# Block products by Strassen's scheme for the dense projections of a hybrid decoder step on one core

## The chip, the cores and the metric

The kernel runs on one core of a Trainium2 chip. The metric is the device time of one launch in microseconds; the time given for a kernel is the median of its runs. A profile is one execution of the program, whose span is read from the trace. Engines are named as the profile names them: PE (matrix multiplication, with PEld for its weight loads), DVE (vector), ACT (scalar activation), POOL (GpSimd) and SP (the queue that issues most DMA).

## The reference, cut to what matters

The computation is one inference step of a decoder with two layers. There are 2048 prompt tokens and 8 x 4 = 32 sample tokens, with D_MODEL = 1024. Everything is float32.

```python
def even_mixer(h, w_in, b_fox, lb, hgrn_gain, w_out, hgrn_s0, fox_attend):      # layer 0
    proj = h @ w_in                                                              # 1024 x 4100
    qa, fa, ia, ga, qb, kb, vb, gb, fb = _split(proj, [A_WIDTH] * 4 + [B_WIDTH] * 4 + [B_HEADS])
    f = lb + (1.0 - lb) * jax.nn.sigmoid(fa)
    o_a, s_a = gated_linear_chunked(ha(qa), ha(1.0 - f), ha(ia), ha(jnp.log(f)), hgrn_s0)
    o_a = head_rmsnorm(o_a, hgrn_gain) * jax.nn.silu(ga)
    log_fb = jax.nn.log_sigmoid(fb + b_fox)
    o_b = fox_attend(hb(qb), kb_h, vb_h, log_fb) * jax.nn.silu(gb)
    return jnp.concatenate([o_a, o_b], axis=-1) @ w_out, ...                     # 1024 x 1024

def odd_mixer(h, w_in, w_gate, b_gate, gla_gain, w_out, gla_s0):                 # layer 1
    q, k, v, g, r = _split(h @ w_in, ...)                                        # 1024 x 3088
    log_f = jax.nn.log_sigmoid(r @ w_gate + b_gate) / GLA_GATE_NORMALIZER
    o, s = gated_linear_chunked(hk(q) * C_KEY_DIM ** -0.5, hk(k), hv(v), hk(log_f), gla_s0)
    return (head_rmsnorm(o, gla_gain) * jax.nn.silu(g)) @ w_out, s               # 1024 x 1024

def run_trunk(x, ...):
    for l in range(2):
        x = x + mixer(rmsnorm(x, norm[l]), ...)
    return rmsnorm(x, final_norm), ...
```

The prompt's forgetting attention ("fox") is causal over its own 2048 tokens; a sample's looks back on 2048 cached tokens of a paged cache. The four dense products, w_in and w_out of both layers, are what the change is about.

## The kernel before, in words

**Stages.** The prompt is taken in two halves of 1024 tokens; the 32 sample tokens ride with half 0. `phase_even` runs the input projections of layer 0 for half 0 and then half 1, mixed with the linear attention of its heads (`lin_attn`). `phase_fox` runs the forgetting attention. `phase_odd` runs, for each half, the output projection of layer 0, the norm, the input projections of layer 1 with their linear attention, and the output projection of layer 1, and at the end the final norm.

**Units.** A dense product is cut into units of 256 output columns: 16 in the even layer's input, 4 in its output, 12 in the odd layer's input, 4 in its output. Each runs once for each half, 72 runs in all. Half of the units are token-major (`proj_tm`, L491): 128 tokens are the stationary operand, 256 weight columns move, and the result has tokens on partitions. The others are feature-major (`proj_fm`, L482): 128 weight columns are stationary and the tokens move, in three segments of 352 in half 0 (1024 + 32 tokens) and two of 512 in half 1.

**Three products.** Both operands are kept as a float16 high part and low part; `mm3` (L476) multiplies high x high, high x low and low x high into one sum in PSUM. A unit has 8 such steps along the 1024 inputs.

```python
    def mm3(self, ps, lh, rh, first, last):
        nc.tensor.matmul(ps, lh[0], rh[0], start=first, stop=False)
        nc.tensor.matmul(ps, lh[0], rh[1], start=False, stop=False)
        return nc.tensor.matmul(ps, lh[1], rh[0], start=False, stop=last)
```

**Weights.** `half_unit` (L315) has four steps: fetch the float32 columns by DMA; `measure` their largest value (DVE, L292); derive a power of two as `scale`; and `split` them into a high and a low part. Of the four parts of a unit, two have their low part made by DVE (L346) after one ACT operation (L345), two by POOL (L353) after two of ACT (L351, L352). The split is made anew in each half. `later_unit` measures the 20 units of the later projections during even half 1. `staged` (L1070) runs the units in order and, as products go by, takes the steps of the next three units.

**Activations.** `act` is one tile of 128 partitions x (high, low) x 8 x 1056 float16, in a single buffer. It is filled by `norm_groups` (L408: row scaling L428 on DVE, transposes on PE, then high part L473 on ACT and low part L474 on DVE) or, for the output projections, by `y_pieces` and `y_to_act` (L1632 on ACT, L1633 on DVE) from the attention outputs `yT` in DRAM. `handover` (L452) interleaves this with the last unit of the old and the first unit of the new activations.

**Sample tokens in token-major units.** `few_rows` (L510) multiplies the 32 tokens in four column strips of PE, each with two of the eight steps; ACT and DVE add up the four strips (L525, L527).

**Order of work.** `mux` weaves two generators by costs in nanoseconds that each step yields; a scheduler then settles each engine's order. SP issues nearly all DMAs in order. PSUM has three buffers (`pj`) for projections.

Of the kernel before, what the change touches and what calls it, by code (L numbers as in the profile page):

```python
# [19 lines left out]
P = 128  # L20
# [10 lines left out]
WU = 272  # L31
LAG_N = 2
ASK = 0
# [6 lines left out]
EWR = 3  # L40
# [4 lines left out]
TAG1 = "o"  # L45
# [8 lines left out]
WSPLIT = 4  # L54
FOX_S = 411000.0
# [5 lines left out]
YPOOL = (2, 6)  # L61
# [4 lines left out]
SCALE = 128.0 ** -0.5  # L66
LEVELS = (1, 2, 4, 8, 16, 32, 64)
# [46 lines left out]

class Parts(tuple):
# [6 lines left out]
class Kern:  # L122
# [6 lines left out]
    def consts(self):  # L129
# [17 lines left out]
        self.kc, self.n_kc, self.scales = cp.tile([P, 184], F32, name="kc"), 0, {}  # L147
        self.vmax = cp.tile([P, NPG], F32, name="vmax")
# [8 lines left out]
        self.x1d = dp.tile([NTOK, D], F32, name="x1d")  # L157

# [85 lines left out]
    def gain_scale(self, g, pps, tag, nm):  # L244


        out = self.kcol(2)
        self.power2(self.spread(g, pps, tag, nm), 2.0**8, out)
        self.nc.vector.tensor_scalar(g, g, out[:, 0:1], None, ALU.mult)
        return out  # L250

    def kcol(self, n=1):
        self.n_kc += n
        assert self.n_kc <= 184
        return self.kc[:, self.n_kc - n : self.n_kc]
# [28 lines left out]
    def unit_scale(self, key, parts, rm, pool, pps, nm, undo, k):  # L284
# [3 lines left out]
        def measure():  # L288
            if key in self.scales:
                return  # L290
            for a, r in enumerate(parts()):
                nc.vector.tensor_reduce(rm()[:, a : a + 1], r, mybir.AxisListType.XY, ALU.max,  # L292
                                        apply_absolute_value=True)
            nc.vector.reduce_max(rm()[:, WSPLIT:], rm()[:, :WSPLIT], axis=mybir.AxisListType.X)

        def scale():
            if key in self.scales:
                return
            sc = self.scales[key] = self.kcol(3)
            self.power(rm()[:, WSPLIT:], 2.0**14, sc, pool, pps, nm)  # L300
            if undo is not None:
                self.last_scale = nc.vector.tensor_scalar(sc[:, 2:3], sc[:, 1:2], undo[:, 1:2], k, ALU.mult, ALU.mult)
# [3 lines left out]
    @staticmethod  # L306
    def sources(w, cols, h):

        for a in range(WSPLIT):
            off = 0  # L310
            for c, n in cols:
                yield a, off, n, w[a * h * P : (a + 1) * h * P, c : c + n].rearrange("(k p) c -> p k c", p=P)
                off += n

    def half_unit(self, pool, pps, w, cols, key, nm, undo=None, k=1.0, also=(), raw=("wr", WU), scaler=None):  # L315
# [1685 lines left out]
```

## Time and profile before

| | us |
|---|---|
| median of 3 runs | 2388.81 |
| range of the runs | 2383.19 to 2390.0 |
| the profiled execution, span | 2392.4 |
| PE busy | 2294.1 |
| DVE busy | 1417.9 |
| ACT busy | 1107.5 |
| POOL busy | 753.7 |

The profiled execution's own time is that of its span; it lies 3.6 us above the median of the runs. Busy times are sums of the records of an engine and may overlap between engines. Matmuls are pipelined, so that each record of one (0.27 us with 256 columns, for instance) is longer than the distance to the next; distances are read from start times. The stages stand in the trace at about 0 to 435 us (even half 0), 435 to 869 (even half 1), 869 to 1325 (fox), 1325 to 1780 (odd half 0 and the output projection before it), 1780 to 2180 (the same of half 1) and 2180 to 2392 us (output projections of layer 1 and the final norm).

### The profile page before, as it was taken

The numbers are of one execution on the slowest core, as the hardware profiler recorded it, in microseconds if no ns is written. First come the engines' busy times: TensorE is split into PE (matmuls) and PEld (weight loads), VectorE is DVE, ScalarE is ACT, GpSimd is POOL, SyncE is SP. The second block draws the span as 40 slices with busy tenths as digits, with TensorE's granted clock in tenths as the row PEclk, the third lists the DMA queues.
The fourth block names the chain that finished last, engine by engine and source line by source line (L and its number), as shares of the span: only waits on it lengthen the run. The fifth ranks groups of instructions, "written<-read, shape, count | busy, mean of one in ns | idle before, by whom it ended". The sixth has DMA issues, their size and how long they took to land. (4 is left out here: it accounts for less than half of the span.)

```text
span 2392.4 us, 58667 instructions
## 1 busy us (share of the span) xinstructions
PE 2294.1 (96%) x23324; PEld 1633.7 (68%) x23324; DVE 1417.9 (59%) x3347; ACT 1107.5 (46%) x2458; POOL 753.7 (32%) x843
## 2 busy tenths in 40 slices
PE   6999999999999999999999999999999999999998
PEld 5677677864655875655446876777778766666887
DVE  7566556446655548666767463665675645557554
ACT  5334343342333226556667454535543635545333
POOL 2233222112212225234556211432452222322322
PEclk9999999999999999999999999999999999999999
DMA  6231234535541267676874632122156312114453
GB/s 198 63 88 58 81 113 142 175 92 143 149 136 43 85 192 258 223 251 203 270 241 134 213 109 58 46 81 86 50 151 196 111 41 70 43 59 159 154 192 147
DMA packets 297013, 317.24 MB, mean 133 GB/s; under 512 B 39730, under 2 KB 241011, under 8 KB 296739
## 3 DMA queue, kind: packets, MB, share of 16 engines
q1 hardware_dynamic: 295234, 308.98, 41.1%
q8 instruction: 183, 3.00, 0.5%
q0 software_dynamic: 1504, 4.52, 0.5%
q14 instruction: 92, 0.75, 0.1%
HBM read 242.31 MB, written 71.11 MB: 131 GB/s over the span
## 5 line engine op out<-in xcount | busy, mean ns | idle before, releaser
L480 PE MATMUL pt_o<-w_o,act 128*128 128x256 f16 x1024 | 280.5, 274 | 3.1 <-DVE act L1633 2.9
L478 PE MATMUL pt_o<-w_o,act 128*128 128x256 f16 x1024 | 280.7, 274 | 1.3 <-ACT sg1C L534 1.1
L479 PE MATMUL pt_o<-w_o,act 128*128 128x256 f16 x1024 | 280.5, 274 | 1.0 <-POOL w_o L353 1.0
L480 PEld LDWEIGHTS <-act 128*128 128x128 f16 x2304 | 226.6, 98 | 36.1 <-issue 4.6
L478 PEld LDWEIGHTS <-act 128*128 128x128 f16 x2304 | 226.6, 98 | 36.0 <-ACT act L473 4.0
L479 PEld LDWEIGHTS <-act 128*128 128x128 f16 x2304 | 226.7, 98 | 32.4 <-issue 2.9
L478 PE MATMUL pt_Cv<-w_Cv,act 128*128 128x256 f16 (+1 forms) x512 | 140.3, 275 | 1.7 <-ACT act L473 0.9
L644 POOL TENSOR_TENSOR kA<-kA,fA 128x512 f32<-128x512 f32 (+1 forms) x56 | 79.8, 1425 | 192.6 <-PE gl_A L610 143.0
L479 PE MATMUL pt_Cv<-w_Cv,act 128*128 128x256 f16 (+1 forms) x512 | 140.0, 274 | 0.0
L480 PE MATMUL pt_Cv<-w_Cv,act 128*128 128x256 f16 (+1 forms) x512 | 139.7, 274 | 0.0
L1241 ACT ACTIVATE L<-L,nm,kc 128x512 f32<-128x512 f32 (+3 forms) x160 | 118.2, 741 | 36.9 <-DVE nm L1239 27.2
L644 POOL TENSOR_TENSOR kC<-kC,fC 128x512 f32<-128x512 f32 (+1 forms) x56 | 81.8, 1461 | 148.2 <-PE gl_C L610 101.3
L1249 POOL TENSOR_SCALAR L<-L,nm 128x512 f32<-128x512 f32 (+3 forms) x160 | 98.8, 631 | 70.8 <-DVE nm L1245 28.6
L1276 ACT ACTIVATE th<-pt 128x512 f16<-128x512 f32 (+3 forms) x159 | 80.7, 527 | 59.8 <-PE pt L1269 58.9
L1277 DVE TENSOR_TENSOR tl<-pt,th 128x512 f16<-128x512 f32 (+3 forms) x159 | 94.4, 609 | 20.3 <-ACT th L1276 19.0
L1269 PE MATMUL pt<-ident,L 128*128 128x128 f32 x544 | 91.3, 280 | 4.9 <-DVE tl L1277 2.4
L1269 PEld LDWEIGHTS pt<-ident,L 128*128 128x128 f32 x544 | 66.7, 143 | 32.4 <-DVE tl L1277 9.1
L1393 PEld LDWEIGHTS pkt<-ident,pgcache_fox_k 128*128 128x128 f32 x512 | 58.1, 141 | 44.4 <-issue 25.6
L1393 PE MATMUL pkt<-ident,pgcache_fox_k 128*128 128x128 f32 x512 | 76.1, 279 | 4.7 <-DVE kts L1397 2.0
L478 PE MATMUL pt_Av<-w_Ai,act 128*128 128x256 f16 x256 | 70.9, 277 | 1.9 <-ACT act L473 1.9
L479 PE MATMUL pt_Av<-w_Ai,act 128*128 128x256 f16 x256 | 70.7, 276 | 0.4 <-DVE w_Ai L346 0.4
L478 PE MATMUL pt_Bk<-w_Bk,act 128*128 128x256 f16 x256 | 71.0, 277 | 0.0
(952 smaller groups left out, 6738.3 us busy)
## 6 DMA issues: line engine op xcount, KB each, us to landing
pgcache_fox_k<-in_cache_fox_k SPq DMA_DIRECT2D x128, 256.0 KB, 4.2
pgcache_fox_v<-in_cache_fox_v SPq DMA_DIRECT2D x128, 256.0 KB, 4.2
yr<-yT SPq DMA_DIRECT2D x16, 1024.0 KB, 7.4
nx<-in_x_prompt SPq DMA_DIRECT2D x16, 512.0 KB, 5.4
wr_Aqf<-in_w_in_even SPq DMA_DIRECT2D x64, 128.0 KB, 3.2
wr_o<-in_w_out_even SPq DMA_DIRECT2D x32, 256.0 KB, 4.5
wr_Cv<-in_w_in_odd SPq DMA_DIRECT2D x32, 256.0 KB, 3.8
wr_Cqk<-in_w_in_odd SPq DMA_DIRECT2D x64, 128.0 KB, 2.8
```

The lines of the kernel that those rows point to most:

```text
L478: nc.tensor.matmul(ps, lh[0], rh[0], start=first, stop=False)
L479: nc.tensor.matmul(ps, lh[0], rh[1], start=False, stop=False)
L480: return nc.tensor.matmul(ps, lh[1], rh[0], start=False, stop=last)
L644: nc.gpsimd.tensor_tensor(kv[:, :, 0], kv[:, :, 0], t1.to_broadcast([P, nb, w]), ALU.mult)
L1241: self.last_exp = nc.scalar.activation(lt[:, :w], lt[:, :w], AF.Exp, bias=nm[:, 0:1], scale=ib, accum_out=nm[:, 2 + j : 3 + j])
L1249: nc.gpsimd.tensor_scalar(lt[:, :w], lt[:, :w], nm[:, 1:2], 2.0**14, ALU.mult, ALU.mult)
L1269: nc.tensor.transpose(pt[:, w : w + P], rows[b][s // 4][0][:, (s % 4) * P : (s % 4 + 1) * P], self.ident)
L1276: nc.scalar.activation(th[:, a:w], pt[:, a:w], AF.Copy),
L1277: nc.vector.tensor_tensor(tl[:, a:w], pt[:, a:w], th[:, a:w], ALU.subtract)))
L1393: nc.tensor.transpose(pk[:, j * P : (j + 1) * P], pgs[j][:, h * P : (h + 1) * P], self.ident)
```

## The change

All units are computed as 2 x 2 block products with seven block multiplications instead of eight. The 1024 inputs are split in two halves of 512, the 256 output columns in two of 128, and the 1024 tokens in two of 512.

- **Activations** are kept as seven block sums, `act0` to `act6`, each 128 x (high, low) x 4 x 512 float16, again in one buffer each. `norm_pairs` and `y_pairs` take the place of `norm_groups`, `y_pieces` and `y_to_act`: they work on a pair of token tiles, one from each half of the tokens (tile j and j + 4), make the sums on DVE and POOL, and split all seven. The gain of the norm is now applied to the rows, from a row tile (`gain_rows`).
- **Weights**: `made` fetches, measures and scales a unit as before, forms three further block sums (three on POOL and one on DVE, in place), and splits seven blocks: ACT makes the scaled values (4 operations) and the high parts (7), DVE five low parts, POOL two. Each block (256 KB) is also stored in DRAM (`wc`). `kept` loads the seven blocks back. A unit is made only once: the 16 even units in even half 0, where they are used at once; the other 20 in even half 1 by `later`, a step each 2050 ns of planned work. The other 56 runs use `kept`.
- **Products**: `seven` runs the seven products into three PSUM tiles. A tile's sum grows on by further products after it was read once: each of the four output blocks is read twice or once (HOLD: write; ADD: add to what is there; WHOLE: alone), seven reads a unit. `put` gives ADD to DVE and the others to ACT; output units add all on DVE.
- **Matmuls**: a token-major unit has 7 x 4 x 4 x 3 matmuls with 128 moving columns, a feature-major one 7 x 4 x 3 with 512.
- **Sample tokens** no longer ride with the others in feature-major units: `few_rows` runs them in column strips in all 36 units of half 0, 60 matmuls of 128 columns, `few_sum` adds up the strips, and feature-major units transpose the sums.
- **Order**: units at a change of activations run in two groups of token tiles (`split`), so that one pair of tiles can be rewritten while the other is still read. The even layer has one buffer less of `c4`, 14 of weight blocks, and `kc` has 256 columns.

`phase_fox` is as before. The core of the diff, cut:

```diff
+    def made(self, pool, pps, w, cols, key, undo=None, k=1.0, raw="wr", tag="w0", store=True):
...
+        def block(i, src, eng):
+            b = pool.tile([P, 2, 4, wd], F16, tag=tag, name=f"w_{key}_{i}")
+            nc.scalar.activation(b[:, 0], src, AF.Copy)
+            self.last_split = eng.tensor_tensor(b[:, 1], src, b[:, 0], ALU.subtract)
+            W[i] = b
+            if store:
+                if i == 0:
+                    self.wc[key] = self.dp.tile([7, P, 2, 4, wd], F16, name=f"wc_{key}")
+                nc.sync.dma_start(self.wc[key][i], b)
...
+            def second():
+                block(1, b21, V)
+                G.tensor_tensor(b11, b12, b11, ALU.subtract)
...
+            def fifth():
+                block(4, b12, G)
+                V.tensor_tensor(b21, b21, b22, ALU.subtract)
...
+    def kept(self, pool, key, tag="w0"):
...
+            def one(i):
+                src = self.wc[key]
+                W[i] = pool.tile(list(src.shape[1:]), F16, tag=tag, name=f"wk_{key}_{i}")
+                self.nc.sync.dma_start(W[i], src[i])
...
+    def seven(new, prod, ev, cost, few=()):
...
+        for i, (t, m, n, kind) in enumerate((("a", 0, 0, HOLD), ("b", 0, 0, ADD), ("a", 0, 1, HOLD), ("c", 1, 1, HOLD),
+                                             ("a", 1, 1, ADD), ("c", 0, 1, ADD), ("a", 1, 0, WHOLE))):
+            first = t not in sums
+            if first:
+                sums[t] = new()
+            for half in prod(sums[t], i, first):
+                if half:
+                    yield Mid(cost / 2)
...
+            ev(sums[t], m, n, kind)
+            yield cost / 2
+
+    def put(self, dst, ps, c, kind):
+        if kind == ADD:
+            self.nc.vector.scalar_tensor_tensor(dst, ps, c, dst, ALU.mult, ALU.add)
+        else:
+            self.nc.scalar.activation(dst, ps, AF.Copy, scale=c)
...
+                for k in range(4):
+                    for x, j in enumerate(js):
+                        self.mm3(ps[:, x], [act[i][:, y, k, j * P : (j + 1) * P] for y in range(2)],
+                                 [W[i][:, y, k] for y in range(2)], first and k + x == 0, k == 3, skip_group_check=True)
...
+    def y_pairs(self, hf, layer, act, pool):
...
+                def split(i, src):
+                    h, l = (act[i][:, x, :, j * P : (j + 1) * P] for x in range(2))
+                    self.last_y = nc.scalar.activation(h, src, AF.Copy, scale=sy)
+                    nc.vector.scalar_tensor_tensor(l, src, sy, h, ALU.mult, ALU.subtract)
+
+                for i, src in ((0, a), (1, b), (6, d)):
+                    split(i, src)
+                    yield 0
+                self.block_sums(a, b, c, d)
+                for i, src in ((3, d), (2, a), (4, c), (5, b)):
+                    split(i, src)
+                    yield 0
```

1121 lines of the change are left out of this document (642 added, 479 removed).

## The prediction

> **What bounds the kernel now.** I read the page's header and busy shares, a table by stage, the waits of PE, the timelines of PE where its rate is set, and the groups of DVE.
>
> ```profile
> span 2392.4 us, 58667 instructions
> PE 2294.1 (96%) x23324; PEld 1633.7 (68%) x23324; DVE 1417.9 (59%) x3347; ACT 1107.5 (46%) x2458; POOL 753.7 (32%) x843
> DVE  7566556446655548666767463665675645557554
> 0.00:435.00 435.00, 408.76 (x4637) 299.61 (x4638) 270.13 (x653) 177.38 (x413) 126.31 (x140) 0.97 0.37 111
> 435.00:869.00 434.00, 428.20 (x4496) 290.94 (x4494) 238.14 (x548) 142.50 (x320) 87.54 (x74) 1.00 0.38 112
> 869.00:1325.00 456.00, 428.67 (x3051) 258.87 (x3049) 309.42 (x947) 284.72 (x640) 219.63 (x329) 0.97 0.71 231
> 1325.00:1780.00 455.00, 436.41 (x4859) 334.34 (x4857) 261.53 (x534) 229.15 (x480) 145.58 (x123) 1.00 0.31 96
> 1780.00:2180.00 400.00, 395.21 (x4117) 279.67 (x4118) 218.26 (x434) 194.33 (x408) 113.75 (x110) 1.00 0.28 87
> 2180.00:2392.00 212.00, 196.87 (x2175) 170.24 (x2173) 120.38 (x235) 79.40 (x200) 60.91 (x68) 0.97 0.52 172
> PE spr_Aqf L279 <- DVE kc L261: 6.8, 1, 6.8
> ```
>
> PE is at work 96% of the span, in every stage (even half 0, even half 1, fox, odd half 0, odd half 1, the last output units; columns: length, then busy time of PE, PEld, DVE, ACT, POOL, granted clock, DMA share, GB/s). Its largest single wait is 6.8 us. DVE is second, 70% to 80% in its fullest slices, 62% in the first stage (270 of 435). So fewer PE microseconds shorten the kernel until DVE, the next engine, is late.
>
> PE's price is the distance from one matmul's start to the next:
>
> ```profile
> 867.90 0.27 PE L478 MATMUL pt_Bv<-w_Bv,act 128*128 128x256 f16 x1
> ...
> 870.96 0.27 PE L479 MATMUL pt_Bv<-w_Bv,act 128*128 128x256 f16 x1
> 1699.50 0.31 PE L478 MATMUL pf_C03q<-act,w_Cqk 128*128 128x352 f16 x1
> ...
> 1701.59 0.31 PE L480 MATMUL pf_C03q<-act,w_Cqk 128*128 128x352 f16 x1
> 679.81 0.38 PE L478 MATMUL pf_A12f<-act,w_Aqf 128*128 128x512 f16 x1
> ...
> 683.48 0.38 PE L480 MATMUL pf_A12f<-act,w_Aqf 128*128 128x512 f16 x1
> 936.92 0.22 PE L478 MATMUL s<-h_k,h_q 128*128 128x128 f16 x1
> 936.98 0.22 PE L479 MATMUL s<-l_k,h_q 128*128 128x128 f16 x1
> 937.03 0.22 PE L480 MATMUL s<-h_k,l_q 128*128 128x128 f16 x1
> L480 PEld LDWEIGHTS <-act 128*128 128x128 f16 x2304 | 226.6, 98 | 36.1 <-issue 4.6 <-DVE act L1633 4.1
> 1355.02 0.77 PE pS_o L522 x24
> ```
>
> 28 steps in 3.06 us: 0.109 us at 256 columns. 14 in 2.09: 0.149 at 352. 17 in 3.67: 0.216 at 512. At 128 columns only triples show, 0.055 to 0.06, each with its own weight load; I take 0.056. The load's record lasts 98 ns, but at 256 columns a new one starts every 109.
>
> **PE's work.** There are 36 units of 256 output columns, each run for two token halves; half of the 72 runs keep tokens as weights (token-major), half feature columns. A token-major run has 192 matmuls of 256 columns, 21.0 us; after, 7 x 4 x 4 x 3 = 336 of 128 columns, 18.8: 36 x -2.2 = -79. A feature-major run of half 0 has 144 of 352, 21.5 us; after, 84 of 512, 18.1: 18 x -3.4 = -61. In half 1, 96 of 512, 20.7, become the same 18.1: 18 x -2.6 = -47. Against this stand the sample tokens, which rode in the 352 columns: now 36 strip groups of 60 matmuls with 128 columns. One of 24 with 256 took 0.77, so half of 0.77/24 each, 0.96 a group, 34.6 in all; the 18 of before took 13.9: +21. Transposes of their sums +4, the wider units' few columns +2. PE in sum: **-160**. As the counts of the built program show 12,096 matmuls of 128x128 and 3,024 of 512, this work does go. In even half 0 it is 6 x -2.2, 10 x -3.4, +11 for the strips and +2, -34; in half 1 6 x -2.2 and 10 x -2.6, -39.
>
> The Trainium skill, "TensorE: Matmul & The Clock Gate", section "Back-to-back issue gap", gives a sustained stream of weight loads and matmuls about 81 ns each at 128 columns and 131 at 512. It speaks against this change: by it the token-major runs would be 12,096 x (81 - 56) = 302 us longer, an estimate. The trace disagrees with its figure at 512 (216 ns) and has a stream at 128 in triples only; the rule is what stands beside rival C.
>
> **DVE's work.** Rows for the new and the old operations:
>
> ```profile
> L346 DVE SCALAR_TENSOR_TENSOR w_o<-wr_o,kc,w_o 128x512 f16<-128x512 f32 x32 | 34.4, 1087 | 7.5 <-ACT w_o L345 7.3
> L346 DVE SCALAR_TENSOR_TENSOR w_Cv<-wr_Cv,kc,w_Cv 128x512 f16<-128x512 f32 x12 | 15.2, 1270 | 3.5 <-ACT w_Cv L345 3.5
> L346 DVE SCALAR_TENSOR_TENSOR w_Bk<-wr_Bk,kc,w_Bk 128x512 f16<-128x512 f32 x8 | 6.1, 774 | 0.4 <-ACT w_Bk L345 0.4
> L474 DVE SCALAR_TENSOR_TENSOR act<-nt,g_odd,act 128x256 f16<-128x256 f32 x64 | 28.8, 477 | 4.4 <-ACT act L473 3.8
> L428 DVE TENSOR_SCALAR row<-row,rsr_n 128x1024 f32<-128x1024 f32 x8 | 6.0, 753 | 3.3 <-DMA x1d<-row 3.0 <-POOL rsr_n L405 0.3
> L1829 DVE SCALAR_TENSOR_TENSOR fx<-fx,rsr_f,gb 128x1024 f32<-128x1024 f32 x8 | 10.3, 1285 | 5.8 <-POOL rsr_f L405 5.8
> L1633 DVE SCALAR_TENSOR_TENSOR act<-yr,kc,act 128x512 f16<-128x512 f32 x48 | 39.0, 845 | 16.9 <-ACT act L1632 16.6
> L1670 DVE SCALAR_TENSOR_TENSOR xo<-pt_o,kc,xo 128x512 f32<-128x512 f32 x32 | 24.0, 749 | 34.4 <-PE pt_o L480 30.3 <-DMA xo<-in_x_prompt 3.1 <-PE py_C L582 0.5
> L527 DVE TENSOR_TENSOR few_o<-few_o,pS_o 32x256 f32<-32x256 f32 x24 | 10.0, 417 | 1.7 <-ACT few_o L525 1.0
> ```
>
> The same weight subtraction takes 774, 1087 or 1270 ns; I take 1087, the most numerous, and keep 1270 for the range. Weights: 36 units x 6 (five low parts, one sum) = 216 against 72 x 2 + 2: 70 more, +76. Norms: per half 36 reads of 512 from PSUM at 0.749 and 8 row products with the gain at 1.285, 37 us, against 32 x 0.477 + 8 x 0.753 = 21: +16, four times. Attention outputs: per half 40 operations at 0.845, 34, against 12 and small change, 11: +23, four times. Evacuations: three additions in 56 runs and three more in 16 output runs, 216 x 0.749 = +162. Few rows: 54 more x 0.417 = +22. In all some +416, to about 1830.
>
> By stage: even half 0 is 270 + 64 x 1.087 (16 units x 6 less 16 x 2) + 48 x 0.749 + 16 + 30 x 0.417 = 404, against PE's new stage length of 435 - 34 = 401. Even half 1 makes the 20 later units: 238 + 88 x 1.087 (20 x 6 less 16 x 2) + 36 + 16 = 386 against 434 - 39 = 395. Odd half 0 comes to about 305 against 421, odd half 1 to 260 against 362, the last stage to 180 against 195. So DVE and PE are level in the first two stages. An engine that bounds can reach the 96% that PE has now: 404/0.96 = 421 and 386/0.96 = 402, **+27** together.
>
> **Changing the activations.** They are single buffered and are now rewritten in pairs of token tiles while a unit run in two column groups still reads the other pairs. At an attention handover PE has half a unit of the old and half of the new, 19 us, while DVE needs 34 and about 10 of evacuations: 25 late, four times. At the two odd norms PE has a unit and a half, 28 us, against 37 + 10 less 5 that can go ahead: 14 each. At the even one, 19: 23. In all 150 at most; at least nothing, since linear attention of the half before is mixed in. Nothing in the trace tells how much that covers; I take half, **+75**.
>
> **The start** asks for the gain rows, two row products and all four scalings before the first block:
>
> ```profile
> L351 ACT ACTIVATE wr_o<-wr_o,kc 128x512 f32<-128x512 f32 x30 | 21.3, 719 | 46.5 <-DMA wr_o<-in_w_out_odd 26.4 <-DMA wr_o<-in_w_out_even 20.1
> ```
>
> 3 x 0.719 more ACT, 2 x 0.53 for the row products, and the later halves of the first pair, 0 to 15 us: **+8**.
>
> **New waits I cost at nothing.** Products grow on in the same PSUM tile, so an evacuation must end within one other product, 48 x 0.056 = 2.7 us, where it had a whole group.
>
> ```profile
> 302.71 0.31 PE L480 MATMUL pf_A03q<-act,w_Aqf 128*128 128x352 f16 x1
> 303.06 0.56 ACT L851 ACTIVATE qA<-pf_A03q,kc 128x352 f32<-128x352 f32 x1 [5.77 <-PE pf_A03q L480]
> wr_o<-in_w_out_even SPq DMA_DIRECT2D x32, 256.0 KB, 4.5
> SPq L594 <- DVE y_C L593: 128.2, 30, 15.4
> SPq L327 <- DVE w_Cv L346: 126.1, 8, 30.0
> L353 POOL TENSOR_TENSOR w_o<-wr_o,w_o 128x512 f16<-128x512 f32 x32 | 44.0, 1393 | 35.4 <-ACT w_o L352 33.7 <-PE kt_C L723 1.6
> ```
>
> This one ends 0.6 us after its matmul; the cover is ACT's and DVE's slack, and a queue of three DVE operations of 1 us takes it away: four places in each of 72 runs. Blocks: seven of 256 KB a run, loaded a unit (18.8 us) ahead, and landing in 4.5. Even half 1 moves 112 x 0.434 = 49 MB now, loses 17 of raw weights, and loads 16 x 1.84 and stores 20 x 1.84: 98 MB in 395 us, 250 GB/s, which the fox stage nearly has now (231 at a share of 0.71). The stores of blocks stand in SP's queue, wait there for DVE's or POOL's subtraction, and hold later units' block loads: SP waited 15.4 and once 30.0 us in one place before, and the second would hold PE 11 us; with DVE on time, zero. POOL does 36 x 5 at 1.393 = 251 against 72 x 2 = 201, and is nowhere near full; ACT grows by some 60.
>
> **Sum**: 2392.4 - 160 + 75 + 27 + 8 = 2342 of the profiled span. Its span is 3.6 above the median of 2388.81, so **2339 us**.
>
> **Rivals.** A: DVE's growth lies beside PE all through, as linear attention fills the handovers: 2392.4 - 160 + 8 - 3.6 = 2237. For it speaks that DVE is under 80% in every slice now. B, slower: DVE sets the pace in the first two stages and at each handover. If its subtractions take 1.27, as for w_Cv, the stages come to (404 + 18)/0.96 = 440 and (386 + 22)/0.96 = 425, +69; with the handovers in full 2392.4 - 160 + 69 + 150 + 8 - 3.6 = 2456. Evacuations and block stores are then late behind DVE's queue, and PE waits in the even stages. It decides from about 95% of DVE's share there. For it: the spread from 774 to 1270. The Trainium skill, "SBUF — State Buffer", section "Who interferes with whom", says that DVE and GpSimd share a port pair under an exclusive lock; the spread of one shape agrees, and POOL's work grows. C: weight loads bound the stream at 128 columns. At the 98 ns of their record 12,096 x 0.042 = +508 on the forecast: 2847. Against it: two triples' steps of 0.055. D: that the products aren't fewer is excluded by the counts above.
>
> **Chances.** Forecast 0.51, A 0.21, B 0.20, C 0.08. The forecast's own range is 2275 to 2390. Measurement can tell 0.3%, 7 us; of the forecast 0.46 lies faster, 0.02 within, 0.03 slower; of B 0.03 is within and 0.02 faster, as its handovers may be covered in part. Faster 0.69, same 0.05, slower 0.26. The range, 2235 to 2445, leaves out C, B's upper part and a little below A.
>
> **What would show it.** Right: spacing of 0.056 in token-major products; DVE near 1830 us in all and over 90% in the even stages; PE's idle time at the changes of act, ended by DVE writing act blocks. A is right if PE stays at 96%; B if PE's waits for DVE spread over all runs of the even stages; C if token-major spacing is 0.08 or more. Wrong in another way: PE waiting for DMA of blocks, or evacuations by ACT.

## The result, and the profile after

The changed kernel takes 2591.09 us (median of 4 runs, 2586.95 to 2597.42) against 2389.4 for the kernel before in the same set: a ratio of 1.084, with a 95% interval of 1.081 to 1.087. Forecast was 2339, in a range of 2235 to 2445. The changed kernel is 202 us slower than the one before, where a gain was forecast, and its time lies above the range.

The page of the changed kernel:

```profile
span 2595.6 us, 72434 instructions
PE 2248.4 (87%) x29144; PEld 1625.3 (63%) x29144; DVE 1813.9 (70%) x3995; ACT 1163.2 (45%) x2533; POOL 881.5 (34%) x901
DVE  8787688667777776856667866565795645569476
```

Its table by stage (columns as in the prediction; a stage begins where the first products of its own kind start, and the second bound, 551, lies in a change of activations in which the products of both halves alternate from 547.8 to 554.5):

```profile
0.00:551.00 551.00, 445.51 (x6150) 310.42 (x6151) 421.25 (x819) 248.79 (x532) 229.34 (x203) 0.93 0.46 146
551.00:1028.50 477.50, 395.57 (x4958) 274.02 (x4956) 356.54 (x653) 224.49 (x455) 203.97 (x152) 0.92 0.65 210
1028.50:1458.70 430.20, 397.47 (x2788) 231.95 (x2786) 309.51 (x962) 278.01 (x625) 200.81 (x312) 0.98 0.70 228
1458.70:1904.40 445.70, 414.19 (x6361) 313.46 (x6359) 291.48 (x656) 170.21 (x377) 98.29 (x88) 0.97 0.39 121
1904.40:2347.40 443.00, 400.52 (x5556) 309.44 (x5556) 266.09 (x543) 163.10 (x358) 93.28 (x85) 0.96 0.42 126
2347.40:2595.60 248.20, 195.17 (x3346) 186.00 (x3343) 169.03 (x368) 78.63 (x190) 55.78 (x63) 0.90 0.56 175
```

PE's share fell from 96% to 87%, DVE's rose from 59% to 70%; no stage has DVE over 77%, and only two slices of 65 us reach 90%. With the same kind of bounds the stages of before last 475, 408, 427, 448, 426 and 208 us. So, with even half 1 taken from its very first product (475.6 us before, 547.8 after), the two even stages are 72 and 73 us longer, the fox stage 3, odd half 0 is 2 shorter, odd half 1 17 longer and the last stage 40.

The matmuls did get cheaper:

```profile
2567.60 0.22 PE L565 MATMUL pt_o<-wk_o,act 128*128 128x128 f16 x1
...
2570.05 0.22 PE L566 MATMUL pt_o<-wk_o,act 128*128 128x128 f16 x1
```

These are 44 steps in 2.45 us: 0.056 each, every one with its own weight load. If each matmul of a trace is counted at the usual undisturbed distance of its kind, PE's work is 2051 us before and 1873 after: some 177 less. (This count, called PE's pure work below, is an estimate from all start times; by what is taken as the usual distance, the saving comes out at 175 to 185.) What is left of the span, pauses and slow stretches, grew from 342 to 722 us. The waits of PE show with whom:

```profile
PE pt_o L565 <- DVE xo L1876: 25.4, 16, 4.2
PE pt_o L565 <- DVE row L1883: 21.1, 15, 11.0
PE gl_A L754 <- DVE qA L787: 20.7, 12, 3.6
PE gl_C L754 <- DVE qC L787: 15.5, 12, 6.4
PE nt L491 <- DVE nx L468: 11.9, 2, 10.8
PE o_A L908 <- DVE Sx L914: 9.4, 7, 3.4
PE pS_Bq L604 <- DVE few_Bq L669: 9.2, 2, 4.6
```

Columns: us in all, times, longest. Before, the largest entry was one wait of 6.8 us. Now there are many short ones: for evacuations (L1876, L1883), for linear attention (L787, L914), for norms (L468) and for sums of sample tokens (L669). All that are shown end with DVE. Added up over all entries, PE's waits grew from 86 to 334 us, of which 257 end with DVE, 46 with ACT and 25 with POOL.

One change of activations shows what such a wait is. The windows run across the last but one handover, into the output units; the timeline behind it is DVE's shortly after 2360, with the matmul that waited:

```profile
2340.00:2360.00 20.00, 15.66 (x260) 13.28 (x258) 18.99 (x32) 8.72 (x17) 6.43 (x4) 0.86 0.31 96
2360.00:2380.00 20.00, 12.23 (x310) 11.19 (x308) 18.65 (x36) 5.72 (x9) 3.71 (x4) 0.80 0.53 142
2380.00:2400.00 20.00, 9.35 (x171) 8.20 (x168) 18.46 (x29) 10.74 (x24) 6.18 (x5) 0.66 0.13 33
2400.00:2420.00 20.00, 17.82 (x314) 16.72 (x312) 9.30 (x22) 2.62 (x9) 1.42 (x2) 1.00 0.66 188
```

```profile
2362.65 0.65 DVE L789 TENSOR_TENSOR fC<-fC 128x256 f32<-128x256 f32 x1
2363.21 0.42 DVE L680 SCALAR_TENSOR_TENSOR sg1C<-th_C,sg1C 128x256 f32<-128x256 f32 x1
2363.55 1.75 DVE L1825 SCALAR_TENSOR_TENSOR act<-yr,kc,act 128x512 f16<-128x512 f32 x1
2365.22 0.41 DVE L680 SCALAR_TENSOR_TENSOR sg1C<-th_C,sg1C 128x256 f32<-128x256 f32 x1
2365.56 0.41 DVE L680 SCALAR_TENSOR_TENSOR sg0C<-th_C,sg0C 128x256 f32<-128x256 f32 x1
2366.00 0.48 DVE L1876 SCALAR_TENSOR_TENSOR xo<-pt_o,kc,xo 128x256 f32<-128x256 f32 x1
2366.54 0.22 PE L565 MATMUL pt_o<-wk_o,act 128*128 128x128 f16 x1 [3.49 <-DVE xo L1876]
```

For 60 us DVE is busy 92% to 95%, and PE 78%, 61% and 47%. PE stood still for 3.49 us before 2366.54, as the sum that it was to go on with had not been read. In DVE's queue the end of one operation and four whole ones of other work stand ahead of that addition (xo): linear attention, gates, and a block of the new activations. And PE's granted clock falls with PE's idleness, 0.86, 0.80, 0.66.

### The profile page after: what moved, and what is told of

Its sections match the earlier page's. It is cut to its first block, busy times and chain, and to the rows that moved or that the text cites. A ratio compares the mean times of both kernels' runs of the same rounds, so it can differ in the third digit from the quotient of the medians.

```text
span 2595.6 us, 72434 instructions
## 1 busy us (share of the span) xinstructions
PE 2248.4 (87%) x29144; PEld 1625.3 (63%) x29144; DVE 1813.9 (70%) x3995; ACT 1163.2 (45%) x2533; POOL 881.5 (34%) x901
## 5 line engine op out<-in xcount | busy, mean ns | idle before, releaser
L566 PEld LDWEIGHTS <-act 128*128 128x128 f16 x4032 | 409.6, 102 | 82.4 <-issue 76.8
L567 PEld LDWEIGHTS <-act 128*128 128x128 f16 x4032 | 408.3, 101 | 23.1 <-DVE act L1825 7.4
L565 PEld LDWEIGHTS <-act 128*128 128x128 f16 x4032 | 408.3, 101 | 18.3 <-issue 3.2
L565 PE MATMUL pt_o<-wk_o,act 128*128 128x128 f16 x1792 | 325.3, 226 | 48.7 <-DVE xo L1876 25.4
L567 PE MATMUL pt_o<-wk_o,act 128*128 128x128 f16 x1792 | 324.0, 226 | 5.9 <-DVE act L1825 5.9
L566 PE MATMUL pt_o<-wk_o,act 128*128 128x128 f16 x1792 | 325.2, 226 | 0.0
L565 PE MATMUL pt_Cv<-wk_Cv,act 128*128 128x128 f16 (+1 forms) x896 | 161.0, 223 | 7.8 <-ACT rr L596 6.3
L567 PE MATMUL pt_Cv<-wk_Cv,act 128*128 128x128 f16 (+1 forms) x896 | 160.4, 223 | 2.2 <-DVE act L497 2.2
L566 PE MATMUL pt_Cv<-wk_Cv,act 128*128 128x128 f16 (+1 forms) x896 | 160.9, 223 | 0.0
L1824 ACT ACTIVATE act<-yr,kc 128x512 f16<-128x512 f32 x112 | 77.5, 718 | 113.8 <-PE pt_o L566 27.2
L1825 DVE SCALAR_TENSOR_TENSOR act<-yr,kc,act 128x512 f16<-128x512 f32 x112 | 93.3, 852 | 9.8 <-ACT act L1824 9.4
L1464 PE MATMUL pt<-ident,L 128*128 128x128 f32 x544 | 92.1, 281 | 8.8 <-POOL L L1444 4.4
L1883 DVE SCALAR_TENSOR_TENSOR row<-pt_o,kc,row 128x128 f32<-128x128 f32 x224 | 66.4, 343 | 44.4 <-PE pt_o L567 43.9
```

Source lines behind the costliest of these rows:

```text
L565: nc.tensor.matmul(ps, lh[0], rh[0], start=first, stop=False, **kw)
L566: nc.tensor.matmul(ps, lh[0], rh[1], start=False, stop=False, **kw)
L1464: nc.tensor.transpose(pt[:, w : w + P], rows[b][s // 4][0][:, (s % 4) * P : (s % 4 + 1) * P], self.ident)
L1825: nc.vector.scalar_tensor_tensor(l, src, sy, h, ALU.mult, ALU.subtract)
L1883: nc.vector.scalar_tensor_tensor(row[:, cs], ps[:, x], undo, row[:, cs], ALU.mult, ALU.add)
```

## The experiments

Unless it is said otherwise, each time is one run, and "less" and "more" are against the changed kernel's 2591. The kernel before took 2387 to 2400 beside them, and over all sets its runs lie up to 17 us apart, so that smaller differences between single runs are not read. Four theories were put against each other: **D**, DVE's added work as such makes PE wait; **W**, DVE stands still behind raw weights that have not landed; **S**, the growing sums leave too little time to read them; **H**, at the changes of activations DVE has more to do than PE's other work covers.

### Measures that wait for nothing

```diff
-                nc.vector.tensor_reduce(rm[:, a : a + 1], t["raw"][:, a * h : (a + 1) * h].rearrange("p k n c -> p k (n c)"),
+                nc.vector.tensor_reduce(rm[:, a : a + 1], self.ident.unsqueeze(1).to_broadcast([P, 4, P]),
```

> The four reductions that measure a unit's weights read a constant tile instead of the fetched weights, so DVE does the same work but never stands still behind weights that have not landed (the scale is then the constant's). Theory W (late weights hold DVE's queue, and PE with it): DVE's idle time behind these fetches, some 90 us in the two even stages, goes, and the time falls by 50 us or more, to 2540 or less. Theory D (it is the amount of DVE work) and theory S (it is the short time in which a sum must be read): no more than 15 us, 2575 to 2600.

Measured: 2540.9, 50 less, 22 of it in even half 0 and 26 in even half 1. W holds for this part: with DVE's work nearly unchanged (1795 us against 1814), taking its stand-still away gave 50 us.

### DVE's low parts of weight blocks by ACT

```diff
-            self.last_split = eng.tensor_tensor(b[:, 1], src, b[:, 0], ALU.subtract)
+            if eng is nc.vector:
+                self.last_split = nc.scalar.activation(b[:, 1], src, AF.Copy)
+            else:
+                self.last_split = eng.tensor_tensor(b[:, 1], src, b[:, 0], ALU.subtract)
```

> The five low parts of a unit's weight blocks that DVE makes are written by ACT as plain copies of the block instead (the subtraction is left out); DVE loses 180 operations of about 1 us, nearly all in the even stages, and ACT gains as many of 0.6 us. Theory D: the even stages lose most of the 130 us by which they are longer than before, and the time falls to 2450 to 2500. Theory W: 2560 to 2590. Theory S: 2550 to 2590, as evacuations on DVE wait a little less.

Measured: 2535.2, 56 less (even stages 32 and 43 less, the next three 4 to 5 more each); DVE 1647 us, 167 less. That lies in none of the three ranges, and is less than D had promised: a microsecond of DVE's work is worth a third of one here, and weight subtractions alone are not the cause.

### No reads of sums that grow on

```diff
+            if kind != HOLD:
-            ev(sums[t], m, n, kind)
+                ev(sums[t], m, n, kind)
...
-            self.nc.vector.scalar_tensor_tensor(dst, ps, c, dst, ALU.mult, ALU.add)
+            self.nc.vector.tensor_scalar(dst, ps, c, None, ALU.mult)
```

> The three reads of a unit of sums that grow on afterwards (kind HOLD) are left out; the three additions stay on DVE, as a scaling of the same size. Outside the output units DVE's work is unchanged, ACT loses three operations a unit, and three of four places a unit go where PE needs a sum read within 2.7 us; output units also lose three DVE operations. Theory S: PE's waits for evacuations, 99 us in all, mostly go, and with them pauses that lower the clock: 2470 to 2510. Theory D: only the output units' 48 operations and less ACT count: 2550 to 2580. Theory W: 2580 to 2600.

Measured: 2570.7, 20 less. S's forecast of 80 us or more fails: PE's waits for ACT's evacuations fell from 28 to 3 us, but those for operations of linear attention on DVE rose from 72 to 93. With a deadline taken away, PE came sooner to the next thing that DVE owed it.

### Strips added up by PE

```diff
-        nc.scalar.activation(r, ps[:TS], AF.Copy)
-        for j in range(1, 4):
-            nc.vector.tensor_tensor(r, r, ps[j * TS : (j + 1) * TS], ALU.add)
+        nc.scalar.activation(r, ps, AF.Copy)
...
+                    self.nc.tensor.matmul(ps, self.strip, t["sum"].rearrange("p n c -> p (n c)"), start=True, stop=True)
```

> The four strips of the sample tokens are added up by one or two PE products with a stacked identity instead of three DVE additions a unit: 108 operations of 0.42 us less on DVE, all in half 0, and PE's waits for them (18 us in the first stage) go. Theory D: 40 to 60 us less, 2530 to 2550, since the place is short and often waited for. Theories W and S: 20 us less at most, 2570 to 2590.

Measured: 2593.4, no change, though DVE has 46 us less and PE's waits for the sums of sample tokens, 20 us before, are gone. PE's pure work grew by some 9. D had promised 40 to 60 us and misses here: these 46 us of DVE's work brought nothing that can be seen beside 9 us more of PE's.

### Low parts of activations left zero

```diff
-                    nc.vector.scalar_tensor_tensor(l, src, sy, h, ALU.mult, ALU.subtract)
...
-                    r = eng.tensor_tensor(l, src, h, ALU.subtract)
-                    if eng is V:
-                        self.last_v = r
+                    self.last_v = self.last_a
```

> The low parts of the activations' blocks are left zero: 28 DVE subtractions fewer at each change of activations (some 24 us each time), while the seven high parts, the sums and the transposes stay. Theory H (the changes of activations stand in full, as DVE needs longer than PE has work from the other pairs): PE's pauses at the seven changes, some 110 us in the odd stages beyond what was there before, shrink by half or more: 2480 to 2530. Theory D alone (amount of DVE work, anywhere): 200 us less work at the rate of the run without DVE's weight subtractions (56 us for 180) gives 2530 to 2550, spread over a stage. Theory W alone: 2580 to 2595.

Measured: 2524.0, 67 less for 130 us less of DVE's work, the best rate so far; 31 of the 67 in the last stage, which went from 248 to 217, and 10 and 13 in the odd halves. H's range holds, and where the time went fits it: DVE's work at the changes is dearer (0.52 of a microsecond for one) than in the weight blocks (0.33).

### Staggered making of blocks

```diff
         def block(i, src, eng):
+            flush()
             b = pool.tile([P, 2, 4, wd], F16, tag=tag, name=f"w_{key}_{i}")
             nc.scalar.activation(b[:, 0], src, AF.Copy)
-            self.last_split = eng.tensor_tensor(b[:, 1], src, b[:, 0], ALU.subtract)
             W[i] = b
+            lows.append((i, b, src, eng))
```

> The making of weight blocks is staggered by one step: a step makes the high part of its block, the low part of the one before, and only stores the one before that, so that SP's queue no longer stands behind a store whose block DVE hasn't finished, and DVE no longer behind a high part that ACT hasn't. All work is kept. Theory W, with the loop through SP's queue (store waits for DVE, raw weights queue behind the store, DVE's measure waits for them): SP's waits for block stores, some 300 us in the even stages, and DVE's waits for raw weights go, and the time falls by 30 to 50 us, to 2540 to 2560. Theory D: no work goes, 2580 to 2600.

Measured: 2607.6, 17 more with the same work. It tells nothing of W: the waits of SP for these stores stood as they were (the longest 23.4 us against 23.2), so that the settled order on the queues was the same in spite of the order in the code.

### Three edits at once

The edits of the first, second and fifth run of this section together.

> Three edits at once: the measures read a constant tile, DVE's low parts of weight blocks are ACT copies, and the low parts of activations are left zero (low parts of both operands are thus not what they should be). If late weights, DVE's weight work and the changes of activations are the three places, and add up: 2591 less 50, 56 and 60 to 110, 2375 to 2425. If they are one queue, in which only the sum counts, less is left: 2300 to 2350, since DVE comes down to the load of the kernel before. If something else holds PE (the short time for evacuations, linear attention's own chain): 2470 or more.

Measured: 2441.3, 150 less for 301 us less of DVE's work. The three gains (50, 56 and 67, together 173) nearly add. DVE's 1512 us are near the 1418 of before, and yet the kernel is 50 us slower than before with 177 us less of PE's work.

### No additions on DVE

```diff
+            if kind != HOLD:
-            ev(sums[t], m, n, kind)
+                ev(sums[t], m, n, kind)
...
-            self.nc.vector.scalar_tensor_tensor(dst, ps, c, dst, ALU.mult, ALU.add)
+            self.nc.scalar.activation(dst, ps, AF.Copy, scale=c)
```

> As the run without the HOLD reads (2571), and the three additions of a unit are scaled copies on ACT instead of DVE: 168 DVE operations of 0.75 us fewer, 126 us; output units keep their additions. Theory D: the rate of the run without DVE's weight subtractions (56 us for 180) gives 40 us, 2520 to 2540. Theory S (a short wait is what costs, whoever does it): 2560 to 2575, since ACT has as many.

Measured: 2557.2, 14 under the run without HOLD reads; that lies between the two forecasts, nearer to S's, and the 14 are within the scatter. DVE has 115 us less than in that run (1655 against 1770), so that each microsecond of it brought about 0.12. PE's waits for DVE's evacuations went from 57 to 21 us, but those for ACT's, which makes the additions now, from 3 to 26, and those for linear attention on DVE from 93 to 103. That it mattered little which engine had these reads speaks for S here, and against a fixed price of DVE's work.

### The kernel before, with more work for DVE

```diff
-                    nc.vector.scalar_tensor_tensor(lo, r, s, hi, ALU.mult, ALU.subtract)
+                    for _ in range(3):
+                        nc.vector.scalar_tensor_tensor(lo, r, s, hi, ALU.mult, ALU.subtract)
```

> The kernel before, in which each low part of weights that DVE makes is made three times over: 290 operations of about 1.08 us more, 316 us, so that DVE's total comes to some 1735 us, near that of the changed kernel (1814). Units, matmuls, evacuations and changes of activations are as before. Theory D (the amount of DVE work alone makes PE wait): at the rate of the run without DVE's weight subtractions (56 us for 180) 60 to 100 us longer than before, 2450 to 2490. If the kernel before hides it, as its sums have whole groups of time to be read and its weights come three units ahead: 2390 to 2410, and what costs in the changed kernel is that its short deadlines leave DVE no time.

Measured: 2497.6, 104 to 108 more than the kernel before, with 215 us more on DVE (the repeats took 0.74 each). Its page, and the first stage in its table:

```profile
PE 2326.7 (93%) x23324; PEld 1650.7 (66%) x23324; DVE 1632.4 (65%) x3639; ACT 1108.0 (44%) x2458; POOL 775.3 (31%) x843
```

```profile
0.00:506.00 506.00, 456.35 (x5021) 341.31 (x5022) 349.16 (x758) 188.58 (x436) 139.94 (x142) 0.96 0.36 107
```

This is the run that decides for D as a cause. Nothing of Strassen's scheme is in it, its first stage has DVE at 69%, and it is 31 us longer there. In the kernel before, too, half of an added microsecond of DVE comes out at the end, at shares far below full. It is not that the weights come late by the repeats: PE's waits that end with a subtraction of weights come to 6 us. Of all its waits, which grew from 86 to 159 us, those for linear attention on DVE grew from 15 to 39.

### Raw weights from ACT's queue

```diff
-                        nc.sync.dma_start(r[:, ks].rearrange("p k n c -> p k (n c)"),
+                        nc.scalar.dma_start(r[:, ks].rearrange("p k n c -> p k (n c)"),
```

> The float32 weights are fetched from ACT's queue instead of SP's, so that they no longer stand behind stores of blocks that wait for DVE; every other transfer stays. Theory W through SP's queue: DVE's waits for raw weights, some 85 us in the even stages, mostly go, and with them 30 to 50 us as in the run whose measures read a constant: 2540 to 2560. If the weights are late for another reason (their buffer comes free late, as its last reader is late): 2580 to 2600, or more, as ACT then waits for that buffer.

Measured: 2592.5, no change. DVE's waits for raw weights stayed, 95 us (84 before the edit). SP's queue is not why they are late.

### Whole groups in the last units

```diff
-            drain(mux(norms0(), 9000.0, dense(37, 40, groups=split), 56000.0))
+            drain(mux(norms0(), 9000.0, dense(37, 40), 56000.0))
```

> The last three output units run with all four pairs of token tiles in one group instead of two groups of two: a product is 48 matmuls (2.7 us) instead of 24 (1.35), so a sum has twice the time to be read; matmuls are the same, DVE's additions as many by elements, and fewer. Theory S in its sharper form (24-matmul products leave DVE's queue no time): PE's 20 us of waits for xo and row sums in the last stage fall by half, 2575 to 2585. Theory H or D: 2588 to 2597.

Measured over 4 runs: 2604.5, a ratio to the kernel before of 1.088 (1.085 to 1.092), against 1.084 (1.081 to 1.087) for the changed kernel. The sharper form of S falls: twice the time to read a sum gained nothing, and PE's waits for these additions stayed (29 us in the last stage, 27 in the changed kernel).

### Low parts shared with POOL

```diff
-                for i, src, eng in ((2, d, V), (3, c, G), (4, a, G), (5, b, V)):
+                for i, src, eng in ((2, d, G), (3, c, G), (4, a, G), (5, b, V)):
...
+                for x in (a, b, c, d):
+                    nc.scalar.activation(x, x, AF.Copy, scale=sy)
```

> At the changes of activations POOL makes three of the seven low parts instead of two (norms) or none (attention outputs); there ACT first scales the rows in place. Work is kept but for ACT's scaling. Theory H: DVE's part of an attention handover falls from 34 to about 24 us, of a norm by 3: 20 to 30 us less, 2560 to 2575. If POOL's and DVE's operations with two inputs from SBUF stop each other, as one timeline of the changed kernel suggests (a subtraction of 0.74 us takes 1.75 beside a POOL operation), nothing is gained: 2585 to 2605.

Measured: 2609.4, 18 more, at the edge of the scatter: nothing is gained. 64 operations of 0.68 to 0.85 us moved away, some 52 us, but DVE's total fell by 18: the others got longer. That fits operations of POOL and DVE which stop each other. It does not show it, and the added scaling on ACT is in the time as well, so the cause of the 18 us stays open.

### More buffers for stored blocks

The trace of the changed kernel has ACT waiting in the even stages until stored blocks have landed, 96 us in all in even half 1:

```profile
ACT w_o L366 <- DMA wc_o<-w_o: 40.8, 23, 5.9
```

```diff
-            wpool = Pool(w0, {"w0": 14, "lw": 3, "wr": 2, "rm": 2, "pow": 2})
+            wpool = Pool(w0, {"w0": 14, "lw": 5, "wr": 2, "rm": 2, "pow": 2})
```

> The later units' weight blocks have 5 buffers instead of 3 in the even stages; nothing else changes. If ACT's waits for landed stores (96 us in even half 1) hold its evacuations, the raw buffers and through them DVE: even half 1 loses 15 to 30 us, 2560 to 2575. If ACT's waits cost nothing, since it is idle for more than half of the time: 2585 to 2600.

Measured: 2592.0. ACT's waits for stores are gone, even half 1 is 10 us shorter, the fox stage 5 longer, and the end is where it was. ACT's waits cost nothing to speak of.

### Everything out

The three edits at once of above, five buffers for blocks, and the edit of the run without additions on DVE, all in one kernel.

> As the run with three edits (2441; measures from a constant tile, low parts of weights by ACT copies, low parts of activations zero), and 5 block buffers, the HOLD reads left out, and the additions as scaled copies on ACT. DVE comes to about 1350 us, below the kernel before. If DVE's load is what is left (half a microsecond for one, as in the loaded kernel before): some 80 us less, 2350 to 2370. If the short deadlines were an extra cost of their own: 2300 or less, towards the 2237 of rival A. If PE's shorter work has met chains that don't get shorter (linear attention, start, norms): 2400 or more.

Measured: 2383.7. Its page:

```profile
PE 2181.4 (92%) x29144; PEld 1596.9 (67%) x29144; DVE 1352.6 (57%) x3278; ACT 1239.9 (52%) x2713; POOL 832.9 (35%) x883
```

It lies between the ranges. Against the run with three edits it is another 58 us less for 160 of DVE's: the rate is 0.36, and there is no free fall to 2237 with three of a unit's four deadlines gone. And in this kernel, with less DVE work than the kernel before, PE's saving has still brought no more than 15 us against the 2399 of its set.

### The kernel before, with less work for PE, and both

```diff
-    def mm3(self, ps, lh, rh, first, last):
+    def mm3(self, ps, lh, rh, first, last, short=False):
...
+        if short:
+            return
...
-                         [x[:, k, c0 : c0 + n] for x in act], k == 0, k == KT - 1)
+                         [x[:, k, c0 : c0 + n] for x in act], k == 0, k == KT - 1, k in (1, 3, 5))
```

> The kernel before, with the low x high product left out in three of eight steps of every projection: an eighth of its matmuls, about 189 us of PE's work, in each stage as much as the change saves there to within some 5 us. DVE's work is as before. If PE is what bounds the kernel before (the first step of the prediction): 160 to 189 us less, 2205 to 2235. If DVE's and the other engines' chains share the pace (0.5 for DVE, so about 0.5 for PE): 80 to 110 us less, 2285 to 2315.

> The same, and each low part that DVE makes is made three times (DVE some 1630 us). If the loads simply add: the time of the run with less PE work plus 104 us. If a shorter PE leaves DVE less cover: plus 130 us or more.

> The same, with each low part made five times: DVE comes to some 1850 us and PE's matmuls to 189 us less than before, both as in the changed kernel, in the structure of the kernel before. If the two loads are the whole cause: 2540 to 2600, the changed kernel's time. If its structure costs besides (growing sums, single buffered blocks of activations, kept blocks): 2480 or less.

Measured: 2275.8, 2371.3 and 2444.2. The pages, in this order:

```profile
PE 2132.5 (94%) x21920; PEld 1506.3 (66%) x21920; DVE 1410.5 (62%) x3347; ACT 1105.0 (49%) x2458; POOL 758.6 (33%) x843
```

```profile
PE 2161.7 (91%) x21920; PEld 1519.2 (64%) x21920; DVE 1634.2 (69%) x3639; ACT 1104.9 (47%) x2458; POOL 790.4 (33%) x843
```

```profile
PE 2180.3 (89%) x21920; PEld 1528.5 (63%) x21920; DVE 1843.9 (75%) x3931; ACT 1103.4 (45%) x2458; POOL 799.0 (33%) x843
```

PE's pure work is 186 us less in each. Alone it brings 119 us (0.64) against 2394.6, which lies between the two ranges: not 186, and more than half. DVE's 224 us more cost 96, the next 210 cost 73, so that the loads add as forecast. The last of the three runs has the changed kernel's two loads (DVE 1844 against 1814, PE's pure work 1865 against 1873) in the old structure, and takes 2444: 50 us more than the kernel before and 147 less than the changed one. So these two loads turn a gain into a loss, but they are not the whole cause. What the change adds to ACT and POOL is not in this run (60 and 83 us less than in the changed kernel).

### Raw weights fetched a unit earlier

```diff
-            wpool = Pool(w0, {"w0": 14, "lw": 3, "wr": 2, "rm": 2, "pow": 2})
+            wpool = Pool(w0, {"w0": 10, "lw": 3, "wr": 3, "rm": 2, "pow": 2})
...
-                    if j + 2 < len(us) and n in (0, 3, 5):
+                    if n == 0:
+                        for u in (2, 3) if j == 0 else (j + 3,):
+                            if u < len(us):
+                                us[u][0][0]()
+                    if j + 2 < len(us) and n in (3, 5):
```

> Raw weights have three buffers instead of two in the even stages and are fetched one unit earlier; to make room the even units' blocks have 10 buffers instead of 14. If it is the distance from fetch to measure: DVE's waits for raw weights (84 us in the even stages) mostly go, and the time falls by 30 to 50 us, 2540 to 2560. If DVE, once it no longer waits there, only waits elsewhere, or blocks now lack buffers: 2575 to 2600.

Measured: 2540.6, 50 less, the same as with measures that wait for nothing. DVE's largest wait of this kind, in the changed kernel and then in this one:

```profile
DVE rm_o L327 <- DMA wr_o<-in_w_out_even: 12.8, 5, 3.9
```

```profile
DVE rm_o L327 <- DMA wr_o<-in_w_out_even: 8.0, 6, 3.5
```

Over all units they fell from 84 to 36 us. The raw weights were late because they were fetched only a unit ahead of their measure, into two buffers; which of the two counts more was not run. With all of the work kept, this is the fastest form of the change that was run, still 6% behind the kernel before.

## Why the prediction was wrong

**What held.** The spacing of 0.056 us was right, and so rival C is out. The Trainium skill's sustained 81 ns ("TensorE: Matmul & The Clock Gate", "Back-to-back issue gap") did not come up in the 45 matmuls above, each with its own weights. PE's pure work fell by some 177, forecast 160. DVE came to 1814, forecast 1830, and in the even stages to 778, forecast 790; that its share there is 76% and 75%, and not over 90%, is due to the stages having grown. ACT grew by 56, forecast 60; POOL by 128 instead of 50, and stays at 34%. Kept blocks were in time: PE's waits for DMA come to 6 us.

**The step that failed** is the first one: that fewer PE microseconds shorten the kernel one for one until DVE, the next engine, is late, and that DVE hides its work until it needs the 96% that PE has. The runs show neither. With PE at 96%, 186 us less of its work brought 119. With DVE at 59%, 215 us more of its work cost 104 to 108. A reason that fits, though no run isolates it, is that the two engines hand work back and forth, so that each one's time comes out in part, whichever is busier: in the changed kernel PE's products of linear attention (L754) wait 36 us for L787, and L787 waits 20 us for such products before. The rates of the kernel before, 0.64 for PE and 0.4 to 0.5 for DVE, applied to the forecast's own loads would have given -160 x 0.64 + 416 x 0.45 = +85: the right sign, and less than half of the 202. In the changed kernel itself the rate of DVE's work is no constant: next to nothing for the strips, about 0.12 for the additions, 0.33 for the weight blocks, 0.52 at the changes of activations. The term of 27 us for the even stages had them come out 46 us shorter than before; they are 145 longer.

**How the 202 us divide**, by the runs on the kernel before: less PE work -119, DVE's load +168, and +147 between that kernel and the changed one at equal loads of these two; together 196 from the 2394.6 of that set. In the place of the 147 the prediction had 83, for the handovers and the start. By stage the profiled executions differ by 66, 63, -10, -7, 22 and 19 in this last part. The late raw weights are worth 50 when they alone are put right, 46 of it in the even stages. The prediction did not see them: it looked for lateness behind SP's stores, and costed that at zero, rightly by the run with ACT's queue. Part of the rest is the start: the second unit's first matmul comes at 92.1 us, and at 59.7 before, so 32 later, where 8 were forecast. And DVE's load in the changed kernel is crowded into the even stages (778 us there, against 712 in the run with equal loads).

What the rest is stays open, and the run with everything out shows how much. It has the matmuls of the changed kernel, and DVE's work is 58 us less than in the run with less PE work alone; no measure of it waits for raw weights, it makes no low parts of activations, and it has one of four deadlines left. Yet it takes 2383.7, and that run 2275.8: 108 us more in the new structure. ACT has 135 us more there and POOL 74, the start is late (the second unit's first matmul comes at 79.7 us, against 60.4), and units and blocks have another order; no run separates these.

**The handovers.** I took half of at most 150. The three stages of the odd layer came out at 446, 443 and 248, where PE's saving alone (34, 38 and 17) would have given 414, 388 and 191: 144 us late in these alone, and the window table above has DVE nearly full and PE waiting at one handover, with no cover from linear attention, which stands in the same DVE queue. How much of the 144 the handovers cost is not shown. The run without low parts of activations takes 54 of it away. And the run with equal loads, which has the old handovers, is 110 late in the same stages, with 820 us of DVE's work there against 727. So half was probably too little, but the term and the price of DVE's load overlap, and the 75 can't be replaced by one measured number.

**Rival B** had the sign, with DVE's queue as the cause and PE's waits spread over the even stages, but it was priced by DVE's being full, from 95% on, and DVE's share there is 76% at most. Its 2456 is 135 short.

**The new deadlines** were put at nothing. PE's waits for evacuations did grow, from 3 to some 100 us, and yet taking three of a unit's four deadlines out gave 20. So most of these waits are places where lateness shows, and not its cause.

**The clock** was in no term. A long pause can be paid again behind it: of the 380 us by which pauses and slow stretches grew, 68 are matmuls that ran at half rate.

## What to carry to other kernels

A share of 96% for one engine does not say that the others' work is free: in a kernel whose engines pass short pieces to each other in fixed order, price an added microsecond of the second engine at what a dummy load on the kernel as it is costs (here 0.4 to 0.5), and a saved one of the first likewise (here 0.64). A scheme that saves 177 us of PE's work for 396 of DVE's was lost at those rates before its handovers were counted. Such rates give the sign and not the size: with both loads at the changed kernel's level, the kernel before was 50 us slower, and the change 202. And look at how far ahead of its first use an input is fetched whenever an in-order queue reads it: a third raw buffer with a fetch one unit earlier was worth nearly as much as taking 167 us of DVE's work away (50 and 56 us).

## What the runs showed of the hardware

One long pause of PE in the changed kernel is followed by matmuls at half rate. After this wait of 4.17 us for DVE the granted clock is 0.50 for 5.6 us, in which a 128-column matmul starts every 0.107 us, and then 1.00 again:

```profile
2461.76 0.26 PE L565 MATMUL pt_o<-wk_o,act 128*128 128x128 f16 x1 [4.17 <-DVE xo L1876]
```

```profile
2461.60:2467.20 5.60, 5.44 (x52) 5.44 (x52) 1.76 (x5) 0.00 (x0) 0.00 (x0) 0.50 0.69 181
2467.20:2472.00 4.80, 4.80 (x89) 4.80 (x87) 2.11 (x4) 1.01 (x2) 0.00 (x0) 1.00 1.09 376
```

In the whole execution the clock is halved for 272 us, against 65 before. The Trainium skill, "TensorE: Matmul & The Clock Gate", section "What's actually happening", has the array throttled to half after at least one idle window of about 3.4 us, and released after at least one busy window as long. This pause of 4.17 us and the 5.6 us behind it agree.

In the handover's timeline above, a subtraction on DVE with two inputs in SBUF (L1825) takes 1.75 us, where the one ahead of it, at 2361.39 us, took 0.74. POOL had begun an operation on SBUF just before, and the subtraction ends 0.55 us after that does:

```profile
2361.39 0.74 DVE L1825 SCALAR_TENSOR_TENSOR act<-yr,kc,act 128x512 f16<-128x512 f32 x1
```

```profile
2363.44 1.31 POOL L788 TENSOR_TENSOR kC<-kC,fC 128x512 f32<-128x512 f32 x1 [7.26 <-DVE fC L789]
```
